# Low parts of the weights of a hybrid encoder layer, granules 10 to 99: an accumulating DMA in place of a subtraction

## The chip, the core and the metric

The kernel runs on one NeuronCore of a Trainium2 chip. The metric is the device time of one execution in microseconds (us), given as the median of several runs. Engines are named as in the profile: PE (matrix multiplication), DVE (vector), ACT (scalar), POOL (GpSimd), SP (the queue that issues most DMAs).

## The reference

One layer of an encoder over 512 tokens of width 1024, in float32. What matters here is that nearly all of the work is activations times large weight matrices:

```python
z, xbc, dt_f, dt_b, q, k, v, gates = split_cols(h @ w_in, IN_SPLITS)
y = ssd_chunked(...forward...) + ssd_chunked(...backward...) + d_skip * xh
branch_ssd = gated_group_rmsnorm(y, z, ssd_norm_g) @ w_br_ssd
branch_attn = windowed_gqa_with_sink(q, k, v, sink) @ w_br_attn
x = x + (g_ssd * branch_ssd + g_attn * branch_attn) @ w_out
x = x + cross_attention(rms_norm(x), rms_norm(mem), w_q, w_kv, w_o)
x = x + (silu(h @ w_gate) * (h @ w_up)) @ w_ffn_out
return rms_norm(x, norm_final_g)
```

## The kernel before

Every weight matrix is cut on the host into **granules** of 128 partitions by 1024 elements (512 KB), numbered 0 to 200 in the order in which the program uses them. The multiplications run on a reduced-precision float format (F32R). To keep float32 accuracy a weight w is split into a high part hi (w rounded to F32R) and a low part lo = w - hi, and an activation likewise. `mac` then issues three matmuls for each 128x128 block: high times high (L140), high weight times low activation (L141) and low weight times high activation (L142). A granule of a projection is 8 blocks, so 24 matmuls of 512 columns. The first of them that reads the low part is the third one.

`load` prepares one granule. SP loads it into a `raw` tile (L122). ACT casts `raw` to the high part `whi` (L130). DVE subtracts, `wlo = raw - whi` (L131). Two ranges deviate: for granules 10 to 18 POOL subtracts (`LO_POOL`), and for granules 79 to 88 DVE also makes the cast (`HI_DVE`, L128). There are two `raw` buffers (`RAWB`), and three each of `whi` and `wlo` (`WB`). So granule g writes the buffers of granule g - 3 and can do so once PE has finished that one. `load` is called so that granule g + 2 is written in the program before the step that uses granule g (`LOOK = 2`).

The stages, by granule: 0 to 27 the key and value projections of the memory (w_xv, w_xk, mixed into the next stage), 8 to 76 the state-space branch (four groups of projections, convolution on DVE and ACT, decay rows masked by POOL at L532 and exponentiated by ACT at L539, and the output projection w_bs), 77 to 92 the windowed attention with its projections (about 515 to 690 us of the profile), 93 to 200 the merge, the cross-attention and the feed-forward part.

Within the block, the order of instructions on each engine is set when the program is built, by a scheduler that works from a timeline of its own. Each engine then runs its instructions in that order, each waiting for semaphores of the others. DMAs that POOL issues stand in POOL's order as well.

Of the kernel before, what the change touches and what calls it, by code (L numbers as in the profile page):

```python
# [9 lines left out]
F32 = mybir.dt.float32  # L10
F32R = mybir.dt.float32r
AF = mybir.ActivationFunctionType
ALU = mybir.AluOpType
AX = mybir.AxisListType

P = 128
# [19 lines left out]
V_MIX, V_XAT, V_MEM, V_FFN, V_FIN = 0, 8, 16, 24, 32  # L36
# [15 lines left out]
HALF = 1  # L52
KVB = 2
LO_POOL = range(10, 19)
HI_DVE = range(79, 89)
ZP = 2
ONE = "mrwomomoo"
TWO = "mzmzm"
# [2 lines left out]
SQ_LAST = 2  # L61
XR = 0
RAWB, WB = 2, 3
EL = (2, 4)


# [7 lines left out]
def bidir_hybrid_layer(ctx: ExitStack, tc: tile.TileContext, io, dbg=None):  # L74
    nc = tc.nc
# [37 lines left out]
    def gcol(c):  # L113
        return vec[:, c:c + 1]


    def load(spec, i):
        src, n = spec
        raw = wp.tile([P, 1024], F32, tag="raw", name="raw", bufs=RAWB)
        for h in range(2 if i < HALF else 1):  # L120
            t = slice(512 * h, 512 * h + 512) if i < HALF else slice(0, n)
            nc.sync.dma_start(raw[:, t], src[:, t])  # L122
        hi = wp.tile([P, 1024], F32R, tag="whi", name="whi", bufs=WB)
        lo = wp.tile([P, 1024], F32R, tag="wlo", name="wlo", bufs=WB)
        for h in range(2 if i < HALF else 1):
            t = slice(512 * h, 512 * h + 512) if i < HALF else slice(0, n)
            if i in HI_DVE:
                nc.vector.tensor_copy(hi[:, t], raw[:, t])  # L128
            else:
                nc.scalar.copy(hi[:, t], raw[:, t])  # L130
            (nc.gpsimd if i in LO_POOL else nc.vector).tensor_tensor(lo[:, t], raw[:, t], hi[:, t].bitcast(F32),  # L131
                                                                     op=ALU.subtract)
        return hi, lo
# [62 lines left out]
    st = {}  # L196
# [287 lines left out]
    def group_scan(g):  # L484
# [124 lines left out]
        for t in range(HPG + LAG3 + 1):  # L609
# [6 lines left out]
            if t >= LAG3 + GLAG and (t - LAG3 - GLAG) % 2 == 0:  # L616
                i = (t - LAG3 - GLAG) // 2
                order += [ga[i]] + el[i + 2:i + 3]
            if t in EL:
                order.append(el[EL.index(t)])  # L620
        cut = order.index(ga[SPLIT]) + 1
# [504 lines left out]
    for i, (fn, gr) in enumerate(steps):  # L1126
        if i == cutat:
            blk.close()
        ahead = LOOK if i >= lead else (i - lead + 4) // 2
        while len(ready) < min(len(specs), taken + len(gr) + ahead):  # L1130
            ready.append(load(specs[len(ready)], len(ready)))
        w = ready[taken:taken + len(gr)]
        taken += len(gr)
        fn(*w)
# [96 lines left out]
```

## Time and profile before

| | |
|---|---|
| median of 3 runs | 1307.06 us (1306.88 to 1308.92) |
| the profiled execution | 1304.91 us, span 1303.1 us |
| PE busy | 1251.0 us, 96% of the span |
| DVE, ACT, POOL busy | 772.1, 564.3, 313.2 us |
| mean granted TensorE clock | 0.991 |

The profile is one execution. Its time is 2.15 us under the median of the runs. The span goes from the first to the last instruction, and 1.8 us of the time lie outside it. Times in rows are counted from the start of the span. A share of busy time is an average over stages that differ: the rows further down are therefore taken from the stretch in which granules 10 to 99 are prepared, 45 to 705 us.

### The profile page before, as it was taken

Reading aid. Unit: us, or ns where it says so; the run is one execution under the profiler, and the core shown is the slowest. Engines: PE = TensorE matmul, PEld = TensorE weight load, DVE = VectorE, ACT = ScalarE, POOL = GpSimd, SP = SyncE. Lnnn points to the kernel's source line nnn. Section 1 sums busy time; section 2 is a strip of 40 time slices with the busy share of each in tenths; the row PEclk is TensorE's granted clock in tenths of the full one; section 3 lists DMA queues with packets and bytes.
Section 4 is the critical chain, followed back from the end, with each engine's and each line's share of the span. In section 5 each row is a group of like instructions: output and inputs, shape, how many; then the busy total and the mean of one; then the engine's idle time right before and its main releaser. Section 6 shows DMA issues by size and latency. Waiting matters only on the chain.

```text
span 1303.1 us, 16244 instructions
## 1 busy us (share of the span) xinstructions
PE 1251.0 (96%) x6076; PEld 1011.3 (78%) x6076; DVE 772.1 (59%) x1226; ACT 564.3 (43%) x1062; POOL 313.2 (24%) x259
## 2 busy tenths in 40 slices
PE   6988999999999999999999999999999999999996
PEld 5776678778778688877667888888888888888886
DVE  5874797677778865688874345675444444432323
ACT  6546655365465232358883234444332222222220
POOL 2344552442671732210000002001111111110001
PEclk9998999999999999999999999999999999999998
DMA  6447364445354232330104333422223222333331
GB/s 228 160 119 196 130 188 148 120 153 141 106 153 137 81 114 80 120 97 33 50 27 139 99 103 107 126 65 65 97 92 98 94 98 95 98 98 94 94 97 65
DMA packets 49614, 143.48 MB, mean 110 GB/s; under 512 B 5120, under 2 KB 8576, under 8 KB 49536
## 3 DMA queue, kind: packets, MB, share of 16 engines
q1 hardware_dynamic: 47248, 138.32, 34.7%
q10 hardware_dynamic: 1584, 2.03, 0.5%
q0 software_dynamic: 704, 2.10, 0.4%
q8 instruction: 48, 0.79, 0.3%
q14 instruction: 30, 0.25, 0.1%
HBM read 137.97 MB, written 4.46 MB: 109 GB/s over the span
## 4 chain that ended last, share of the span: by engine, by line
PE 59%; issue 6%; DVE 2%; ACT 1%; POOL 1%; DMA 0%; DVEq 0%; POOLq 0%; ACTq 0%
PE mm L140 18%; PE mm L142 18%; PE mm L141 18%; PE sb L818 1%; PE sb L805 1%; POOL rsw L717 1%; PE sb L992 1%; PE sa L961 1%; PE sa L777 1%; PE sa L779 0%; PE sb L172 0%; PE sb L572 0%; ACT whi L130 0%; PE sb L155 0%; ACT rsw L716 0%
## 5 line engine op out<-in xcount | busy, mean ns | idle before, releaser
L130 ACT CAST whi<-raw 128x1024 fp32r<-128x1024 f32 (+2 forms) x192 | 198.9, 1036 | 452.3 <-PE mm L141 359.4
L140 PE MATMUL mm<-hh,whi 128*128 128x512 f32 x968 | 382.9, 396 | 11.8 <-DVE cvu L409 11.1
L142 PE MATMUL mm<-hh,wlo 128*128 128x512 f32 x968 | 379.9, 393 | 0.0
L141 PE MATMUL mm<-hl,whi 128*128 128x512 f32 x968 | 379.8, 392 | 0.0
L131 DVE TENSOR_TENSOR wlo<-raw,whi 128x1024 fp32r<-128x1024 f32 (+2 forms) x193 | 238.2, 1235 | 145.0 <-ACT whi L130 135.2
L140 PEld LDWEIGHTS mm<-hh,whi 128*128 128x128 f32 x968 | 182.5, 189 | 52.0 <-issue 8.0
L142 PEld LDWEIGHTS mm<-hh,wlo 128*128 128x128 f32 x968 | 182.4, 188 | 38.9 <-issue 1.8
L141 PEld LDWEIGHTS mm<-hl,whi 128*128 128x128 f32 x968 | 182.7, 189 | 37.1 <-issue 1.1
L539 ACT ACTIVATE rt<-rt,nb 128x128 f32<-128x128 f32 x256 | 78.8, 389 | 67.4 <-POOL rt L532 67.3
L187 POOL TENSOR_TENSOR sq_acc<-sq_acc,sq 128x512 f32<-128x512 f32 x14 | 24.4, 1744 | 259.0 <-ACT sq L186 259.0
L1045 POOL TENSOR_TENSOR fa<-fa,row 128x512 f32<-128x512 f32 x22 | 39.1, 1779 | 192.3 <-ACT fa L1044 192.3
L140 PE MATMUL mm<-vh,whi 128*128 128x512 f32 (+1 forms) x192 | 71.1, 370 | 6.8 <-DVE cvu L409 2.7
L409 DVE SCALAR_TENSOR_TENSOR cvu<-mm,hcw,cvu 128x510 f32<-128x510 f32 (+1 forms) x96 | 71.4, 743 | 5.3 <-ACT cvu L406 3.8
L140 PE MATMUL mm<-fh,whi 128*128 128x512 f32 (+1 forms) x198 | 72.4, 366 | 0.0
L141 PE MATMUL mm<-fl,whi 128*128 128x512 f32 (+1 forms) x198 | 72.4, 365 | 0.0
L142 PE MATMUL mm<-fh,wlo 128*128 128x512 f32 (+1 forms) x198 | 72.4, 365 | 0.0
L142 PE MATMUL mm<-vh,wlo 128*128 128x512 f32 (+1 forms) x192 | 70.7, 368 | 0.0
L141 PE MATMUL mm<-vl,whi 128*128 128x512 f32 (+1 forms) x192 | 68.8, 358 | 0.0
L532 POOL TENSOR_SCALAR_AFFINE_SELECT rt<-rt 128x512 f32<-128x512 f32 x64 | 47.6, 766 | 67.7 <-DMA rt<-adr 67.5
L1047 DVE TENSOR_TENSOR ft<-fa,mm 128x512 f32<-128x512 f32 x22 | 15.1, 688 | 72.5 <-PE mm L142 70.4
L141 PE MATMUL mm<-ol,whi 128*128 128x512 f32 x128 | 50.0, 391 | 0.0
L142 PE MATMUL mm<-oh,wlo 128*128 128x512 f32 x128 | 50.0, 391 | 0.0
(231 smaller groups left out, 1953.7 us busy)
## 6 DMA issues: line engine op xcount, KB each, us to landing
raw<-in_w_in SPq DMA_DIRECT2D x69, 512.0 KB, 3.5
raw<-in_w_fi SPq DMA_DIRECT2D x44, 512.0 KB, 3.5
rt<-adr SPq DMA_DIRECT2D x32, 512.0 KB, 5.5
ear<-edr SPq DMA_DIRECT2D x32, 256.0 KB, 4.5
raw<-in_w_bs SPq DMA_DIRECT2D x16, 512.0 KB, 3.4
raw<-in_w_fo SPq DMA_DIRECT2D x16, 512.0 KB, 3.5
raw<-in_w_xk SPq DMA_DIRECT2D x8, 512.0 KB, 3.9
raw<-in_w_ba SPq DMA_DIRECT2D x8, 512.0 KB, 3.4
```

The lines of the kernel that those rows point to most:

```text
L130: nc.scalar.copy(hi[:, t], raw[:, t])
L131: (nc.gpsimd if i in LO_POOL else nc.vector).tensor_tensor(lo[:, t], raw[:, t], hi[:, t].bitcast(F32), op=ALU.subtract)
L140: nc.tensor.matmul(acc, wh, xh[:, k0 + k], start=first and k == 0, stop=False)
L141: nc.tensor.matmul(acc, wh, xl[:, k0 + k], start=False, stop=False)
L142: nc.tensor.matmul(acc, wl, xh[:, k0 + k], start=False, stop=last and k == nk - 1)
L187: eng.tensor_tensor(acc, acc, sq, op=ALU.add)
L409: nc.vector.scalar_tensor_tensor(u[:, b], acc[:, a], w5[j], u[:, b], op0=ALU.mult, op1=ALU.add)
L532: nc.gpsimd.affine_select(out=rt[:, d].rearrange("p (c l) -> p c l", c=NCH), in_=rt[:, d].rearrange("p (c l) -> p c l", c=NCH), pattern=[[ ...
L539: nc.scalar.activation(r, r, AF.Exp, bias=st["nb"][:, c, e0:e0 + 1])
L717: nc.gpsimd.tensor_tensor(sw, sw, st["ca"][:, S:2 * S], op=ALU.mult)
L1045: nc.gpsimd.tensor_tensor(a, a, st["row2"], op=ALU.mult)
L1047: nc.vector.tensor_tensor(t, a, st["fp", 2 * j + 1], op=ALU.mult)
```

## The change

Granules 10 to 99 (`LO_DMA`) get their low part in another way. ACT makes the high part as before (now L128). A second ACT instruction (L129) writes the negated value, rounded to F32R in the same way, into `wlo`. Then POOL issues a DMA (L133) that reads the granule a second time from device memory and adds it to `wlo` in place, so that `wlo` becomes w - hi. `LO_POOL` is no longer reached, and `HI_DVE` is emptied, so that the casts of granules 79 to 88 return to ACT. For granule 88 (`CHECKED`) the subtraction is also made on DVE for 256 columns, the two are compared, and the largest squared difference times 1e15 is added to the gain of the final norm. Granules 0 to 9 and 100 to 200 stay as they were.

```diff
-HI_DVE = range(79, 89)
+HI_DVE = range(0)
...
+LO_DMA = range(10, 100)
+CHECKED = 88
...
         hi = wp.tile([P, 1024], F32R, tag="whi", name="whi", bufs=WB)
         lo = wp.tile([P, 1024], F32R, tag="wlo", name="wlo", bufs=WB)
+        if i in LO_DMA:
+            nc.scalar.copy(hi[:, :n], raw[:, :n])
+            nc.scalar.activation(lo[:, :n], raw[:, :n], AF.Copy, scale=-1.0)
+            if i == CHECKED:
+                gap = st["at"].tile([P, 256], F32, tag="gap", name="gap", bufs=1)
+                nc.vector.tensor_tensor(gap, raw[:, 0:256], hi[:, 0:256].bitcast(F32), op=ALU.subtract)
+            nc.gpsimd.dma_start(lo[:, :n], src[:, :n], accum_op=ALU.add)
+            if i == CHECKED:
+
+                worst = st["at"].tile([P, 1], F32, tag="worst", name="worst", bufs=1)
+                nc.vector.tensor_tensor(gap, gap, lo[:, 0:256].bitcast(F32), op=ALU.subtract)
+                nc.scalar.activation(gap, gap, AF.Square)
+                nc.vector.tensor_reduce(worst, gap, axis=AX.X, op=ALU.max)
+                nc.vector.scalar_tensor_tensor(gcol(V_FIN), worst, 1e15, gcol(V_FIN), op0=ALU.mult, op1=ALU.add)
+            return hi, lo
```

The scheduler makes a new order of it. The first place is POOL's queue where granules 10 to 16 are prepared. Before, after the four stores of `vdr`, the low parts are subtractions:

```order
L279 DMA vdr_73<-xw_401 128x512
L131 TENSOR_TENSOR wlo_419<-raw_416,whi_418 128x1024
L131 TENSOR_TENSOR wlo_502<-raw_499,whi_501 128x1024
L131 TENSOR_TENSOR wlo_543<-raw_540,whi_542 128x1024
L259 DMA kdr_72<-xw_571 128x256
L131 TENSOR_TENSOR wlo_577<-raw_574,whi_576 128x1024
L131 TENSOR_TENSOR wlo_625<-raw_622,whi_624 128x1024
```

Of the change, the same place:

```order
L296 DMA vdr_73<-xw_401 128x512
L133 DMA wlo_419<-in_w_xk 128x1024
L133 DMA wlo_503<-in_w_in 128x1024
L276 DMA kdr_72<-xw_574 128x256
L133 DMA wlo_545<-in_w_in 128x1024
L133 DMA wlo_580<-in_w_xk 128x1024
L133 DMA wlo_629<-in_w_in 128x1024
```

Each subtraction has become a DMA that POOL issues, in nearly the same place among the others.

The second place is ACT in the state-space stage, at granules 45 and 46 (`cvu`, `cvt`: the convolution; `xk`: a transposed copy; `zs`, `vh`: the gate). Before:

```order
L130 CAST whi_2412<-raw_2410 128x1024
L406 ACTIVATE cvu_2382<-mm_2357,hcw_412 128x512
L466 COPY xk_2181<-sb_2391 128x4x128
L130 CAST whi_2460<-raw_2458 128x1024
L478 ACTIVATE zs_2441<-mm_2416 128x512
L411 ACTIVATE cvt_2388<-cvu_2382 128x512
```

Of the change:

```order
L128 CAST whi_2447<-raw_2445 128x1024
L423 ACTIVATE cvu_2417<-mm_2392,hcw_412 128x512
L129 ACTIVATE wlo_2448<-raw_2445 128x1024
L483 COPY xk_2213<-sb_2426 128x4x128
L428 ACTIVATE cvt_2423<-cvu_2417 128x512
L128 CAST whi_2496<-raw_2494 128x1024
L495 ACTIVATE zs_2477<-mm_2452 128x512
L129 ACTIVATE wlo_2497<-raw_2494 128x1024
```

Every cast has got a second pass over the granule one ACT instruction behind it.

The third place is DVE at the granule that is compared, where the attention begins (`x1`: the gated branch; `sm0`, `sm1`, `mx`: scores and their maxima), of the change alone:

```order
L132 TENSOR_TENSOR gap_4910<-raw_4904,whi_4906 128x256
L859 SCALAR_TENSOR_TENSOR x1_69<-ts_4901,x1_69 128x512
L798 ISA sm0_4946,mx_4950<-sa_4954,ca_4496 128x256
L798 ISA mx_4950 128x1
L137 TENSOR_TENSOR gap_4910<-gap_4910,wlo_4907 128x256
L798 ISA sm1_4947,mx_4950<-sa_4958,ca_4496 128x256
```

The second `gap` row waits for the DMA of that granule, and three of the four score rows of the first attention block stand behind it.

## Rows read from the trace of the kernel before

**Rows 1.** The page: engines' busy time, and the chain that ended last by engine.
```profile
PE 1251.0 (96%) x6076; PEld 1011.3 (78%) x6076; DVE 772.1 (59%) x1226; ACT 564.3 (43%) x1062; POOL 313.2 (24%) x259
...
PE 59%; issue 6%; DVE 2%; ACT 1%; POOL 1%; DMA 0%; DVEq 0%; POOLq 0%; ACTq 0%
```

**Rows 2.** Stages 45 to 705 us and 585 to 690 us: busy time of engines, clock, DMA.
```profile
core 0: us, PE busy (x) PEld busy (x) DVE busy (x) ACT busy (x) POOL busy (x), PEclk, DMA share, GB/s
45.00:705.00 660.00, 631.95 (x3213) 497.28 (x3213) 486.37 (x823) 348.26 (x751) 230.29 (x196) 0.99 0.40 118
585.00:690.00 105.00, 104.04 (x538) 71.59 (x537) 81.95 (x296) 84.27 (x226) 5.26 (x4) 1.00 0.12 40
```

**Rows 3.** What PE waited for, 45 to 705 us: total, times, longest.
```profile
PE mm L140 <- DVE cvu L409: 13.7, 3, 6.4
PE sb L465 <- DVE xs L412: 2.4, 2, 1.7
...
PE sa L777 <- DVE mx L781: 2.3, 2, 1.9
PE mm L140 <- DVE cvt L642: 2.3, 4, 1.4
...
PE sb L805 <- DVE sm L795: 0.2, 1, 0.2
```

**Rows 4.** Three consecutive matmuls of a projection and the next: start, duration (timeline).
```profile
970.63 0.39 PE L140 MATMUL mm<-hh,whi 128*128 128x512 f32 x1
970.86 0.39 PE L141 MATMUL mm<-hl,whi 128*128 128x512 f32 x1
971.08 0.39 PE L142 MATMUL mm<-hh,wlo 128*128 128x512 f32 x1
971.31 0.39 PE L140 MATMUL mm<-hh,whi 128*128 128x512 f32 x1
```

**Rows 5.** Granule 10: cast, and first matmul of its low part (timeline).
```profile
44.76 1.04 ACT L130 CAST whi<-raw 128x1024 fp32r<-128x1024 f32 x1
51.71 0.28 PE L142 MATMUL mm<-vh,wlo 128*128 128x256 f32 x1
```

**Rows 6.** Granule 11: cast, subtraction on POOL, first matmul of its low part.
```profile
53.35 1.05 ACT L130 CAST whi<-raw 128x1024 fp32r<-128x1024 f32 x1 [2.18 <-PE mm L141]
54.48 2.40 POOL L131 TENSOR_TENSOR wlo<-raw,whi 128x1024 fp32r<-128x1024 f32 x1 [5.78 <-ACT whi L130]
57.24 0.39 PE L142 MATMUL mm<-hh,wlo 128*128 128x512 f32 x1
```

**Rows 7.** Granule 79, cast by DVE, and granule 99: cast, first matmul of low part.
```profile
531.29 0.62 DVE L128 CAST whi<-raw 128x1024 fp32r<-128x1024 f32 x1
534.86 0.39 PE L142 MATMUL mm<-hh,wlo 128*128 128x512 f32 x1
701.14 1.06 ACT L130 CAST whi<-raw 128x1024 fp32r<-128x1024 f32 x1 [3.89 <-PE mm L141]
712.50 0.39 PE L142 MATMUL mm<-hh,wlo 128*128 128x512 f32 x1
```

**Rows 8.** DMA issues: size of each, median us from issue to landing.
```profile
raw<-in_w_in SPq DMA_DIRECT2D x69, 512.0 KB, 3.5
rt<-adr SPq DMA_DIRECT2D x32, 512.0 KB, 5.5
...
kdr<-xw POOLq DMA_DIRECT2D x8, 128.0 KB, 4.5
...
edr<-x SPq DMA_DIRECT2D x1, 128.0 KB, 2.2
```

**Rows 9.** POOL 45 to 705 us, groups by line: busy, mean ns, idle before.
```profile
L532 POOL TENSOR_SCALAR_AFFINE_SELECT rt<-rt 128x512 f32<-128x512 f32 x64 | 47.6, 766 | 67.7 <-DMA rt<-adr 67.5
...
L131 POOL TENSOR_TENSOR wlo<-raw,whi 128x1024 fp32r<-128x1024 f32 x9 | 22.4, 2497 | 25.7 <-ACT whi L130 23.5 <-PE mm L141 2.2
...
L259 POOL DMA_DIRECT2D kdr<-xw x8 | 4.5, 563 | 5.5 <-DVE xw L258 5.3 <-issue 0.2
```

**Rows 10.** The subtraction L131, 45 to 705 us: busy time on DVE and POOL.
```profile
45.00:705.00 660.00, 103.92 (x81) 22.40 (x9) 0.99 0.40 118
```

**Rows 11.** DVE ahead of one of PE's three waits for the convolution (timeline).
```profile
111.84 1.23 DVE L131 TENSOR_TENSOR wlo<-raw,whi 128x1024 fp32r<-128x1024 f32 x1 [1.74 <-ACT whi L130]
112.98 0.74 DVE L409 SCALAR_TENSOR_TENSOR cvu<-mm,hcw,cvu 128x510 f32<-128x510 f32 x1
```

## The prediction

> **What bounds the kernel now.** I read the page's busy times and chain first. PE is busy for 1251.0 of 1303.1 us and carries 59% of the chain that ended last; no other engine carries more than 2% [rows 1]. So the kernel runs at the pace of PE, and another engine matters only where PE waits for it. In the stretch in which granules 10 to 99 are prepared, PE is busy for 631.95 of 660 us and DVE for 486.37, the most of the others [rows 2]. The list of PE's waits there shows how much of the rest is DVE's: eight kinds of waits, of which the first and the last stand in [rows 3], 24.8 us in all, over half of it in three waits for the convolution. That sum is the ceiling of what a freer DVE can give back.
>
> Then I read how early a low part has to be there. PE starts a matmul every 0.227 us (970.63 to 971.31 is three) [rows 4], so a granule of 24 takes 5.44 us. The buffers of granule g come free at the end of granule g - 3. The third matmul of granule g comes two granules and 0.45 us later, at least 11.3 us. Granule 99 shows it: its cast starts at 701.14, as soon as PE lets the buffer go, and its low part is first read at 712.50, which is 10.3 us after the cast's end [rows 7]. Other PE work between two granules makes this longer, and a late cast makes it shorter. I went through the timeline and took for each of the 90 granules the time from the end of its cast to the first matmul that reads its low part; call it A. Granule 10 is the first, with 51.71 - 45.80 = 5.9 us [rows 5], granule 99 the last. The shortest are granule 11 with 2.8 us [rows 6] and granule 79 with 2.95 us [rows 7]. The quartiles are 8.4, 11.0 and 14.9 us. Today the subtraction uses 1.3 us of it on DVE (103.92 / 81) and 2.5 us on POOL [rows 9, 10].
>
> **The change part by part.** *DVE* loses 81 subtractions, 103.9 us [rows 10], and ten casts of 0.62 us like that of granule 79 [rows 7]. What that gives is bounded by 0 and the 24.8 us. Where PE waited 6.4 us for the convolution at 113 us, the subtraction stood directly ahead of it but took 1.23 us of the wait [rows 11]. So I take 1.2 us for each of the three long waits and about 2 us for the short ones: 6 us gained.
>
> *ACT* gets 90 negated copies of the cast's size, 1.04 us each [rows 5], and the ten casts: 90 x 1.04 + 10 x 1.04 = 104 us. Over the stretch it goes from 348 to 452 of 660 us, which PE's work covers. In the attention it is busy for 84.27 of 105 us [rows 2]; there about nine granules bring 9.4 us, and the exponentials that PE waits for stand in the same queue. Bounds 0 and 9.4 us; I take 3 us lost. In the order shown, one other ACT instruction stands between a cast and its negated copy, so the copy costs little more than itself.
>
> *POOL* loses nine subtractions (22.4 us) and gets 90 DMA issues of about 0.563 us each, 50.7 us [rows 9]: from 230 to 259 of 660 us. The issues stand in order behind masks of 0.77 us and sums that wait for others. At 39% busy I take 0.5 us of waiting for each, with bounds 0 and 1. In the order shown for granules 10 to 16 the issues stand where the subtractions stood.
>
> *The comparison* of granule 88 adds five small instructions. Its second DVE row waits for one transfer, with three score rows behind it; the granule has over 12 us until its use and I cost it at nothing. Without that cover it is one transfer, at most some 7 us.
>
> *The accumulating transfer* is the unknown, since no row of before shows one. Call D the time from issue to landing. The nearest rows: 512 KB from device memory, issued by SP, land after 3.5 us; 128 KB issued by POOL need 4.5 us and 128 KB issued by SP 2.2 us [rows 8]. So POOL's way costs some 2.3 us more, which gives 3.5 + 2.3 = 5.8 us for a plain copy of a granule. The add also needs the old content of the tile. Size costs (3.5 - 2.2) us for 384 KB, or 1.7 us for a granule, so a second read in full gives 7.5 us. The low end is 3.5 us, as if POOL's way cost nothing. For the high end I have no row: three reads and writes in turn, each at 3.5 us, would be 10.5 us. The DMA engines are busy for 0.40 of the stretch at 118 GB/s [rows 2]; 47 MB more add 71 GB/s, so their share goes to 0.64, or 0.88 if both reads count. Transfers will meet, as with the 5.5 us of the broadcast rows [rows 8]. I take D = 7.0 us, between 5.8 and 7.5 and nearer to the upper.
>
> The Trainium skill, page "Collectives: The Full Stack", section "The bandwidth ceiling: the fold count and why AG ≠ RS ≠ AR", says that an add inside a transfer costs no time in the adder but two source reads, and so halves the rate; by that rule the upper of the two, 7.5 us, holds. No row here shows such an add.
>
> *The sum of the waits.* A low part now needs the negated copy (1.04), POOL's wait (0.5) and D, 8.5 us in all after the cast. It is late by f = 8.5 - A: for 23 granules, most for 11 (5.7 us), 79 (5.6) and 22 (4.8). Delays do not simply add up. When PE waits at granule g, the casts of the next two already run, so only what exceeds the delay gained since two granules earlier counts: T(g) = the larger of T(g - 1) and T(g - 2) + f(g). Carried over the 90 granules this gives T = 34 us with casts as late as before. For D of 3.5, 5, 6, 8, 10 and 12 us it gives 7, 15, 22, 50, 97 and 154 us. If every cast started as soon as its buffer is free, as granule 99's does, the same sum would be 8 us with D = 7, since the time from free buffer to use is 11.2 us or more for nine granules in ten. The new order lies between: DVE no longer holds up casts and the worst granules were accidents of the old order, but ACT has more to do. I take 20 us, about the middle.
>
> Sum: 20 - 6 + 3 = 17 us, so the profiled execution goes from 1304.9 to about 1322 us. The median lies 2.15 us above that execution: 1307 + 17 = 1324 us.
>
> **The rivals.** (1) *The transfer is hidden.* If D plus POOL's wait stays under about 5 us, or the new order starts the casts early, PE waits 3 to 8 us more at low parts, and the 6 us up to, at best, 15 us of DVE's relief decide: -8 to +2 us, 1299 to 1309. For it: half of the granules have A above 11 us, and the plain load lands in 3.5 us. Against it: POOL's own DMAs land after 4.5 us with a quarter of the bytes [rows 8]. It turns at D of about 5 us.
>
> The Trainium skill, page "DMA: Bandwidth & Descriptors", section "Anatomy of one DMA — SWDGE (gpsimd) path", gives 2.0 us plus the bytes over 436 GB/s for a DMA issued by GpSimd, 3.2 us for a granule as an estimate; by that rule this rival holds. The trace disagrees at the size that it shows: 128 KB take 4.5 us, where the rule gives 2.3.
>
> (2) *The transfer is long.* With D of 10 to 12 us the need exceeds the 11.3 us that two dense granules give, so that PE waits in nearly every projection: 97 to 154 us, 1400 to 1460. For it: both reads and the write could go one after the other, while raw loads share the engines. Against it: the load moves 512 KB within 3.5 us.
>
> (3) *ACT becomes the bound in the attention*, where it goes from 84 to some 94 of 105 us: up to 9.4 us instead of 3, with all else as forecast, 1330. It is inside the forecast's own range.
>
> **How the numbers follow.** The forecast (D of 5 to 9 us, +3 to +65 us) gets 0.46, the hidden transfer 0.32, the long one 0.18, and 0.04 is left for gains and losses that cancel. Within 0.2% (2.6 us) is about what a measurement of this kernel cannot tell from no change. The hidden case falls 0.24 into faster and 0.08 into the same, so: faster 0.24, same 0.12, slower 0.64. The range goes from 1296 us, the hidden case with more of DVE's waits cured, to 1390 us (+83, D of about 9.5), which leaves out most of the long case. The forecast's own range is 1310 to 1372 us.
>
> **What would show it.** L133 issues that land after 6 to 8 us; PE waiting at L142 for DMAs into `wlo`, some 20 us between 45 and 705 us, the most near granules 10 to 13, 22 to 28 and 79; DVE about 110 us and POOL 28 us away from before, down and up; ACT up by 104 us; nothing changed after 720 us. Landings under 5 us, or no such waits, would make it wrong on one side; landings over 10 us on the other.

## The result, and the profile after

The changed kernel takes 1367.74 us (median of four runs, 1359.99 to 1369.8) against 1307.37 us before: a ratio of 1.0447 [1.043, 1.0465], so 60 us slower. The forecast was 1324 us. The sign was right, and the time lies inside the wide range, but the loss is more than three times the 17 us that were forecast.

The page of the profile after: busy times, the DMA queues (packets, MB, share of 16 engines), the chain that ended last, and four of the DMA issues (size, median us to landing).

```profile
PE 1274.1 (93%) x6076; PEld 1026.4 (75%) x6076; DVE 664.5 (49%) x1139; ACT 660.6 (48%) x1163; POOL 348.6 (26%) x340
...
q1 hardware_dynamic: 47248, 138.32, 33.5%
q0 software_dynamic: 13664, 49.29, 19.6%
...
PE 64%; DMA 16%; issue 9%; POOL 5%; DVE 3%; ACT 2%; SPq 0%; POOLq 0%; DVEq 0%; ACTq 0%
...
raw<-in_w_in SPq DMA_DIRECT2D x69, 512.0 KB, 5.1
wlo<-in_w_in POOLq DMA_DIRECT2D x63, 512.0 KB, 7.6
...
rt<-adr SPq DMA_DIRECT2D x32, 512.0 KB, 6.8
```

Read PE first. It runs the same 6076 matmuls as before, yet is busy for 1274.1 us where it was 1251.0 [rows 1]. The span went from 1303.1 to 1365.2 us, 62.1 more: 23.1 us are matmuls that took longer, and 39.0 us are idle time (91.1 against 52.1). So there are two losses, and the forecast had terms for the second kind only. DMA has 16% of the chain now; the chain of before can't be set beside it, since its shares in [rows 1] add up to only 69% of the span. The accumulating transfer lands after 7.6 us, near the 7.0 that were taken; the plain loads, 3.5 us before [rows 8], need 5.1.

What PE waited for, 45 to 765 us, which is the work of 45 to 705 us before (total, times, longest). It answers to [rows 3].

```profile
PE mm L159 <- DMA wlo<-in_w_in: 25.1, 13, 4.6
PE mm L159 <- DMA wlo<-in_w_xk: 9.0, 4, 4.4
PE mm L157 <- DVE cvt L659: 6.7, 4, 3.8
PE sa L577 <- ACT cvu L423: 5.9, 1, 5.9
PE sa L794 <- ACT gap L138: 4.7, 1, 4.7
PE sa L577 <- DVE mt L567: 4.1, 2, 3.3
PE sb L460 <- DVE cf L429: 3.6, 1, 3.6
PE sb L515 <- POOL xw L507: 3.4, 2, 3.2
PE mm L157 <- DVE cvu L426: 1.4, 1, 1.4
```

Seventeen waits for low parts make 34.1 us, and the comparison of granule 88 makes 4.7. The waits for the convolution on DVE fell from 13.7 us to 1.4, but other waits took their place, those of L577 for the masked decay rows above all: 10.0 us in three waits, which were 1.0 us before (45 to 705 us):

```profile
PE sa L560 <- DVE mt L550: 1.0, 2, 0.8
```

Without low parts and comparison, 27.1 us are left of PE's 65.9 idle us in this stretch; before it was 660 - 631.95 = 28.05 in all [rows 2].

The stretch as a whole (to be read beside [rows 2]), and 20 us of it in steps of 5 us: busy times of the engines, granted clock, share of the DMA engines, GB/s.

```profile
core 0: us, PE busy (x) PEld busy (x) DVE busy (x) ACT busy (x) POOL busy (x), PEclk, DMA share, GB/s
45.00:765.00 720.00, 654.07 (x3216) 511.41 (x3215) 379.68 (x737) 445.34 (x854) 266.26 (x278) 0.96 0.73 173
...
125.00:130.00 5.00, 5.00 (x34) 4.08 (x32) 0.69 (x1) 1.97 (x5) 1.73 (x3) 1.00 0.76 234
130.00:135.00 5.00, 0.70 (x5) 0.42 (x4) 1.35 (x2) 5.00 (x12) 3.61 (x5) 0.76 0.75 141
135.00:140.00 5.00, 4.90 (x24) 4.83 (x24) 0.00 (x0) 2.07 (x7) 0.97 (x2) 0.55 0.79 189
140.00:145.00 5.00, 3.03 (x10) 2.02 (x9) 2.85 (x4) 3.06 (x7) 2.29 (x3) 0.79 0.58 147
```

The second loss stands here. PE stood still for nearly all of 130 to 135 us, and in the 5 us that followed it was granted 0.55 of its clock, that is 1.2 GHz nearly throughout, and got 24 matmuls done instead of 34. Reading the windows in steps of 2 us, I found ten such places between 45 and 765 us, each at a wait of PE, and three in the kernel before. The clock that was not granted adds up to 29.0 us against 6.8. Part of that falls into the waits themselves and costs nothing: over the time in which PE was busy it is 23.2 us against 4.9. The difference, 18.3 us, is most of the 22.1 us by which PE's busy time grew in the stretch (654.07 against 631.95); the other 3.8 us stay open. Of the 23.2 us, 9.6 lie at five of the waits for low parts, 2.5 at the comparison and 11.2 at four other waits (5.9, 3.6, 3.3 and 3.8 us in the list above); the 4.9 us of before lie at its three waits for the convolution.

Two of the seventeen waits, from the timeline after: granule 21 (cast, negated copy, a mask on POOL, the issue, PE's wait) and granule 79.

```profile
118.66 1.05 ACT L128 CAST whi<-raw 128x1024 fp32r<-128x1024 f32 x1
119.61 1.06 ACT L129 ACTIVATE wlo<-raw 128x1024 fp32r<-128x1024 f32 x1
...
128.28 1.22 POOL L549 TENSOR_SCALAR_AFFINE_SELECT rt<-rt 128x512 f32<-128x512 f32 x2 [5.83 <-DMA rt<-adr]
129.44 0.87 POOL L133 DMA_DIRECT2D wlo<-in_w_xk  x1
...
135.10 0.58 PE L159 MATMUL mm<-vh,wlo 128*128 128x256 f32 x1 [4.41 <-DMA wlo<-in_w_xk]
...
569.63 1.05 ACT L128 CAST whi<-raw 128x1024 fp32r<-128x1024 f32 x1 [7.57 <-POOL x L660]
570.59 1.05 ACT L129 ACTIVATE wlo<-raw 128x1024 fp32r<-128x1024 f32 x1
...
571.93 0.88 POOL L133 DMA_DIRECT2D wlo<-in_w_in  x1 [2.71 <-ACT wlo L129]
...
580.22 0.80 PE L159 MATMUL mm<-hh,wlo 128*128 128x512 f32 x1 [3.25 <-DMA wlo<-in_w_in]
580.81 0.63 PE L157 MATMUL mm<-hh,whi 128*128 128x512 f32 x1
581.24 0.63 PE L158 MATMUL mm<-hl,whi 128*128 128x512 f32 x1
```

The transfer was quick for granule 21: 5.7 us from issue to use. But its copy was ready at 120.67 and the issue came at 129.44, since POOL's queue stood before a mask that waited for a broadcast row. For granule 79 POOL was prompt (0.3 us); there ACT stood 7.57 us before the cast, the last 4.0 of them with the buffer already free, and the transfer then took 8.3 us. The last two rows show 1.2 GHz behind the wait: a matmul every 0.43 us instead of 0.227 [rows 4].

I did this for all seventeen. Four of 1.3 to 4.4 us (granules 21, 22, 25, 27) had 5 to 9 us in POOL's queue; five (10, 18, 48, 79, 84) had a cast 4 to 7 us after the buffer was free; granule 42 had both. These ten make 26.8 of the 34 us. The ten casts that went back to ACT (granules 79 to 88) have no run of their own; five of the seventeen waits, 9.4 us, stand there.

### The profile page after: what moved, and what is told of

It reads as the page before. It is cut to its first block, busy times and chain, and to the rows that moved or that the text cites. A ratio compares the mean times of both kernels' runs of the same rounds, so it can differ in the third digit from the quotient of the medians.

```text
span 1365.2 us, 16370 instructions
## 1 busy us (share of the span) xinstructions
PE 1274.1 (93%) x6076; PEld 1026.4 (75%) x6076; DVE 664.5 (49%) x1139; ACT 660.6 (48%) x1163; POOL 348.6 (26%) x340
## 4 chain that ended last, share of the span: by engine, by line
PE 64%; DMA 16%; issue 9%; POOL 5%; DVE 3%; ACT 2%; SPq 0%; POOLq 0%; DVEq 0%; ACTq 0%
PE mm L159 19%; PE mm L157 19%; PE mm L158 19%; DMA rt<-adr 7%; DMA wlo<-in_w_in 6%; POOL mt L562 1%; DMA raw<-in_w_in 1%; POOL x L660 1%; PE sb L589 1%; PE sb L1009 1%; PE sa L978 1%; POOL rt L549 1%; POOL wlo L133 1%; PE sb L515 1%; PE sb L835 1%
## 5 line engine op out<-in xcount | busy, mean ns | idle before, releaser
L159 PE MATMUL mm<-hh,wlo 128*128 128x512 f32 x968 | 385.0, 398 | 25.1 <-DMA wlo<-in_w_in 25.1
L147 ACT CAST whi<-raw 128x1024 fp32r<-128x1024 f32 (+2 forms) x112 | 115.2, 1029 | 361.5 <-PE mm L158 312.3
L148 DVE TENSOR_TENSOR wlo<-raw,whi 128x1024 fp32r<-128x1024 f32 (+2 forms) x112 | 134.3, 1201 | 101.8 <-ACT whi L147 97.4
L128 ACT CAST whi<-raw 128x1024 fp32r<-128x1024 f32 x90 | 94.2, 1047 | 138.1 <-PE mm L158 86.5
L133 POOL DMA_DIRECT2D wlo<-in_w_in x63 | 55.1, 875 | 169.8 <-ACT wlo L129 126.3
L129 ACT ACTIVATE wlo<-raw 128x1024 fp32r<-128x1024 f32 x90 | 94.6, 1051 | 0.1
L157 PE MATMUL mm<-vh,whi 128*128 128x512 f32 (+1 forms) x192 | 74.4, 388 | 8.2 <-DVE cvt L659 6.7
L158 PE MATMUL mm<-vl,whi 128*128 128x512 f32 (+1 forms) x192 | 72.0, 375 | 0.0
L549 POOL TENSOR_SCALAR_AFFINE_SELECT rt<-rt 128x512 f32<-128x512 f32 x64 | 43.3, 710 | 80.4 <-DMA rt<-adr 80.4
```

What stands on the lines that cost most here:

```text
L128: nc.scalar.copy(hi[:, :n], raw[:, :n])
L129: nc.scalar.activation(lo[:, :n], raw[:, :n], AF.Copy, scale=-1.0)
L133: nc.gpsimd.dma_start(lo[:, :n], src[:, :n], accum_op=ALU.add)
L157: nc.tensor.matmul(acc, wh, xh[:, k0 + k], start=first and k == 0, stop=False)
L158: nc.tensor.matmul(acc, wh, xl[:, k0 + k], start=False, stop=False)
L159: nc.tensor.matmul(acc, wl, xh[:, k0 + k], start=False, stop=last and k == nk - 1)
```

## The experiments

All but e7, e8, e10 and e12 start from the changed kernel without the comparison (e1). "Idle" is span minus PE busy, each from its own page; PE has 6076 matmuls in every run. "Low parts" is what PE waited for the transfers.

| run | median, us | before, us | ratio | span | PE busy | idle | low parts |
|---|---|---|---|---|---|---|---|
| the change | 1367.74 | 1307.37 | 1.0447 [1.043, 1.0465] | 1365.2 | 1274.1 | 91.1 | 34.1 |
| e1 no comparison | 1361.07 | 1309.19 | 1.0386 [1.0348, 1.0423] | 1360.2 | 1274.1 | 86.1 | 32.8 |
| e2 plain transfer | 1330.79 | 1309.19 | 1.0167 [1.0145, 1.0188] | 1333.4 | 1265.9 | 67.5 | 12.9 |
| e3 nobody waits | 1386.52 | 1309.19 | 1.0593 [1.0576, 1.0609] | 1384.1 | 1282.2 | 101.9 | 0 |
| e4 no second read | 1303.88 | 1309.19 | 0.996 [0.9945, 0.9975] | 1301.6 | 1254.0 | 47.6 | 0 |
| e5 low parts last | 1342.6 | 1309.63 | 1.0254 [1.0236, 1.0272] | 1339.2 | 1265.6 | 73.6 | 21.6 |
| e6 negated on DVE | 1345.97 | 1309.63 | 1.0285 [1.0261, 1.0309] | 1342.2 | 1267.3 | 74.9 | 27.7 |
| e7 granules 56 to 78 | 1319.11 | 1309.63 | 1.0078 [1.0061, 1.0095] | 1317.3 | 1258.5 | 58.8 | 8.1 |
| e8 granules 101 to 198 | 1314.77 | 1309.63 | 1.004 [1.0024, 1.0055] | 1312.8 | 1259.3 | 53.5 | 0.2 |
| e9 16 columns only | 1322.79 | 1307.76 | 1.0113 [1.0098, 1.0128] | 1318.9 | 1257.2 | 61.7 | 12.2 |
| e10 before, low last | 1309.87 | 1307.76 | 1.0014 [1.0, 1.0028] | 1308.9 | 1254.1 | 54.8 | 0 |
| e11 e5 and e6 | 1323.84 | 1307.76 | 1.0123 [1.0108, 1.0138] | 1321.9 | 1261.0 | 60.9 | 10.1 |
| e12 granules 12 to 20 | 1313.46 | 1307.76 | 1.0046 [1.0029, 1.0062] | 1311.4 | 1257.4 | 54.0 | 9.8 |

**e1.** The comparison alone.

```diff
-CHECKED = 88
+CHECKED = -1
```

> The changed kernel without the comparison of granule 88; all else as in the change. Theory A (late low parts: what was lost is PE's own waits for the transfers into the low parts, 33 us, and the granted clock that falls after such waits, about 21 us) gives the comparison the one wait of 4.7 us that PE has behind it in the trace, so 1361 to 1364 us. Theory B (crowded transfers: the second read slows all other transfers, and masks, rows and raw loads come late) says the same here. If the comparison were worth 10 us or more, it would be a cause of its own.

Measured 1361.07 us, as both expected. The comparison costs some 7 us by the medians (8 by the ratios): the wait of 4.7 us and what comes behind it. The size is not sharp, since the runs overlap (1359.99 to 1369.8 with it, 1354.67 to 1365.22 without). By the first read of each low part, PE falls a further 8.1 us behind the kernel before between granules 84 and 99 in the change and 2.2 us in e1, a difference of 5.9.

**e2.** Same order on every engine as e1, same bytes from device memory, no add.

```diff
-nc.gpsimd.dma_start(lo[:, :n], src[:, :n], accum_op=ALU.add)
+nc.gpsimd.dma_start(lo[:, :n], src[:, :n].bitcast(F32R))
```

> As the run without the comparison, with the same order of instructions on every engine, but the transfer that POOL issues writes the granule into the low part instead of adding it, so the low part holds the whole weight. Same issue, same bytes from device memory, no read of the tile. If the add is what makes the transfer long and the DMA engines full, landing falls from 7.6 to about 5 us, the share of the DMA engines from 0.75 to about 0.6, and by theories A and B 20 to 40 us come back: 1320 to 1345 us. If instead the place of the issue in POOL's queue decides (theory C: the issue stands behind masks that wait for broadcast rows, up to 8.8 us after the negated copy), less than 10 us come back: 1352 to 1362 us.

Measured 1330.79 us: 30 us are back, within the 20 to 40 of theories A and B and over the 10 of theory C. The page of e1, and then that of e2:

```profile
q0 software_dynamic: 13664, 49.29, 19.5%
...
raw<-in_w_in SPq DMA_DIRECT2D x69, 512.0 KB, 5.1
wlo<-in_w_in POOLq DMA_DIRECT2D x63, 512.0 KB, 8.0
```

```profile
q0 software_dynamic: 13664, 49.29, 10.8%
...
raw<-in_w_in SPq DMA_DIRECT2D x69, 512.0 KB, 3.7
wlo<-in_w_in POOLq DMA_DIRECT2D x63, 512.0 KB, 4.7
```

With the add the same packets kept the DMA engines busy for 19.5% of 1360.2 us, or 265 us; without it 10.8% of 1333.4, or 144 us. The add makes the same packets 1.8 times as much work for the engines and the landing of a transfer 1.6 times as long (7.7 against 4.7 us, the median of all 90), and the plain loads beside it take 5.1 us instead of 3.7. The low-part waits fall from 32.8 to 12.9 us, PE's busy time by 8.2 us, and all other idle time goes from 53.3 to 54.6 us. So what it costs is in the waits for low parts and in slower matmuls; the slower loads show in no other wait. Two things this run doesn't separate: how much of a transfer's length is the add itself and how much the fuller DMA engines, and the add from the conversion of float32 to F32R inside the transfer, which the edit takes out with it.

The Trainium skill, page "Collectives: The Full Stack", section "The bandwidth ceiling: the fold count and why AG ≠ RS ≠ AR", says of ReduceScatter, a transfer between cores that adds, that the add needs two source reads and that it runs at half the rate of a copy. By the engines' busy time the transfer here comes near that (1.8); by the time to landing it is less (1.6). The skill's page "DMA: Bandwidth & Descriptors", section "Anatomy of one DMA — SWDGE (gpsimd) path", gives 3.2 us (an estimate from its formula) for a plain transfer of this size issued by GpSimd; the trace disagrees, with 4.7 and no landing under 3.7.

**e3.** No reader of the low parts.

```diff
-            return hi, lo
+            return hi, hi
```

> No comparison; negated copies and accumulating transfers as in the change, but the third matmul of granules 10 to 99 reads the high part, so the low part that arrives is not used and no engine waits for it. PE does the same number of matmuls. Theory A: PE's waits for low parts (33 us) and the clock lost behind them are gone, and the time is 1300 to 1318 us. Theory B: the other transfers are still slowed, masks and raw loads are still late, and the time stays at 1335 us or more. The scheduler makes a new order for it, since it no longer sees the wait.

Measured 1386.52 us, slower than the change, which by the letter speaks for theory B. The trace says that it tells nothing of the question. Without a reader the scheduler put the negated copies far earlier. ACT's waits, 45 to 745 us:

```profile
ACT wlo L129 <- DMA raw<-in_w_in: 119.8, 34, 7.7
ACT wlo L129 <- DMA raw<-in_w_bs: 45.5, 13, 7.0
```

ACT stood there for 165 us with its convolution and exponentials in the queue behind. It is a new stall, made by the edit; e5 and e11 take up the question.

**e4.** The transfer alone is taken out.

```diff
-            nc.gpsimd.dma_start(lo[:, :n], src[:, :n], accum_op=ALU.add)
```

> No comparison and no accumulating transfer: the low part keeps the negated high part. Casts and negated copies on ACT as in the change, no subtraction on DVE or POOL. All theories that lay the loss on the transfers (A, B, C) expect it at or under the kernel before: 1296 to 1308 us, the prediction's 6 us of relief less 3 us for ACT being 1304. If the ten casts and ninety negated copies on ACT are what costs (theory D), it stays above 1320 us.

Measured 1303.88 us, a ratio of 0.996. This is what theories A, B and C expected; theory D's load on ACT does not by itself bring 1320 us. Freer DVE and POOL, less ACT's load, are together worth 5 us, where the forecast had 6 - 3 = 3. What ACT's copies cost by themselves the run doesn't show apart from that relief.

**e5.** The same transfers, but a later need.

```diff
 for k in range(nk):
     nc.tensor.matmul(acc, wh, xh[:, k0 + k], ...)
     nc.tensor.matmul(acc, wh, xl[:, k0 + k], ...)
-    nc.tensor.matmul(acc, wl, xh[:, k0 + k], ...)
+for k in range(nk):
+    nc.tensor.matmul(acc, wl, xh[:, k0 + k], ...)
```

> No comparison; in every granule the eight matmuls with the low part are issued after the sixteen with the high part, so that a low part is first read 3.2 to 3.6 us later. Transfers as in the change. Theory A (the loss is PE's waits for late low parts, 33 us in seventeen waits of 0.3 to 4.8 us in the run without the comparison, and the clock that falls after the long ones): most of these waits end, under 10 us are left, and the time is 1312 to 1335 us. Theory B (the second read slows all transfers, so masks, rows and raw loads come late, which this does not change): 1345 us or more.

Measured 1342.6 us, between the two. 18 us came back, but 21.6 us of waits are left, not under 10, most of them at other granules than in e1. (The waits of e1, 32.8 us, are fifteen; seventeen is the number in the change.)

**e6.** The negated copy on another engine.

```diff
-nc.scalar.activation(lo[:, :n], raw[:, :n], AF.Copy, scale=-1.0)
+nc.vector.tensor_scalar(lo[:, :n], raw[:, :n], -1.0, None, op0=ALU.mult)
```

> No comparison; the negated copy is made by DVE instead of ACT, beside the cast and not behind it. Theory D (ACT: its copies make casts late, 4 to 9 us after the buffer is free for granules 10, 42, 48, 79 and 84, and the negated copy ends 2.0 to 4.5 us after the cast's start): the waits for low parts fall from 33 to about 15 us and the time to 1330 to 1345 us. If only the transfer and POOL's queue count, at most the 1.3 us by which the copy ends earlier is gained per wait: 1345 to 1358 us.

Measured 1345.97 us, at the border of the two. 15 us came back, as theory D has it, but the waits fell only to 27.7 us: four of the five over 3 us went, that of granule 79 grew from 3.0 to 5.2 us, and short ones came in. PE's busy time fell by 6.8 us. So only 5 of the 15 us are waits for low parts, and that ACT's copies made the casts late is shown only in part.

**e7.** Part of the change on the kernel before (`HI_DVE` as before).

```diff
+LO_DMA = range(56, 79)
```

> The kernel before, with the accumulating transfer for granules 56 to 78 only (23 of the 90). In the trace of the change PE is as far behind the kernel before at granule 79 (41.5 us) as at granule 56 (41.9), so by theory A, whose waits stand elsewhere, this costs nothing: within 3 us of the kernel before. By theory B in the form that each second read costs the same wherever it is, a quarter of the loss: 13 to 16 us slower.

Measured 1319.11 us, 9.5 us slower: theory A's number was wrong. PE's waits for low parts in it, from the timeline, are 2.7 us at granule 57, 0.9 at 58 and 4.5 at 62. In the full change PE waited for none of these three low parts, which landed 6.0, 1.8 and 2.2 us before their use. I put that down to PE having been held up before; the order of the program differs too, and no run separates the two. Where a chain has waits, the place at which none shows is not one that is free.

**e8.** The last part of the program, with more granules than the change has.

```diff
+LO_DMA = range(101, 199)
```

> The kernel before, with the accumulating transfer for granules 101 to 198 only, the merge, the cross-attention and the feed-forward part (98 granules, more than the change has). PE has no broadcast rows or masks to wait for there, and the DMA engines are busy for 0.30 of it. Theory A with the lead of 11.3 us and a need of 2.0 us for cast and copy, 0.3 for POOL and 6 to 7.6 for the transfer: hidden, within 4 us of the kernel before, with some loss possible in the cross-attention. Theory B in the form that each second read costs the same: 50 us or more slower.

Measured 1314.77 us, 5.1 us slower (3 to 7 by the interval) where theory A had up to 4 and theory B over 50. Two stretches of it, and two DMA issues of its page:

```profile
1000.00:1100.00 100.00, 100.00 (x443) 82.84 (x442) 19.34 (x28) 46.61 (x56) 27.50 (x27) 1.00 0.91 194
1100.00:1200.00 100.00, 100.00 (x442) 82.65 (x441) 15.89 (x23) 44.39 (x53) 26.43 (x27) 1.00 0.90 191
```

```profile
raw<-in_w_fi SPq DMA_DIRECT2D x44, 512.0 KB, 6.5
wlo<-in_w_fi POOLq DMA_DIRECT2D x44, 512.0 KB, 7.6
```

The DMA engines are busier here than in the change (0.91 against 0.73) and loads land after 6.5 us, yet PE is busy throughout at 2.4 GHz. By the first matmul of each granule, PE is 4.2 us behind the kernel before already at granule 100, and until about there every engine has the same order as before; from there to granule 200 the 98 transfers add 3.0 us.

**e9.** The same issue and wait, few bytes.

```diff
-nc.gpsimd.dma_start(lo[:, :n], src[:, :n], accum_op=ALU.add)
+nc.gpsimd.dma_start(lo[:, :16], src[:, :16], accum_op=ALU.add)
```

> No comparison; the accumulating transfer covers 16 of the 1024 columns, so it has the same issue on POOL, behind the same masks, and the same wait of PE, but 1/64 of the bytes (the other columns of the low part keep the negated high part). With POOL's queue alone (theory C: waits of 5 to 9 us in front of the issue for granules 20 to 28 and 41, 42) most of the 13 us of waits of the run with the plain read stay, and the time is 1318 to 1330 us. If the bytes decide (theories A and B: the length of the transfer and the crowding of the DMA engines), it is within 8 us of the run without a second read, 1304 to 1312 us.

Measured 1322.79 us, as theory C expected: 19 us more than without any transfer, though these land after 3.5 us. The timeline of e9 for granule 22:

```profile
126.97 1.06 ACT L129 ACTIVATE wlo<-raw 128x1024 fp32r<-128x1024 f32 x1
...
130.65 1.23 POOL L549 TENSOR_SCALAR_AFFINE_SELECT rt<-rt 128x512 f32<-128x512 f32 x2 [6.24 <-DMA rt<-adr]
...
140.29 1.23 POOL L549 TENSOR_SCALAR_AFFINE_SELECT rt<-rt 128x512 f32<-128x512 f32 x2 [5.05 <-DMA rt<-adr]
141.47 0.86 POOL L133 DMA_DIRECT2D wlo<-in_w_in  x1
...
143.90 0.77 PE L159 MATMUL mm<-hh,wlo 128*128 128x512 f32 x1 [5.35 <-DMA wlo<-in_w_in]
```

The copy was ready at 128.03, the issue came 13.4 us later, and the transfer took 2.4 us. The order of the program is a new one, so not all of the 19 us need be POOL's queue. Of the 12.2 us of waits for low parts, 6.7 stand behind 8 to 13 us in that queue (granules 17, 21 and 22); at granules 11, 48 and 86, 5.5 us, the copy waited at most 0.9 us there. PE's busy time is 3.2 us longer than in e4.

**e10.** e5's edit of the matmuls on the kernel before.

> The kernel before with the low-part matmuls last in each granule, as a control of the run that did this to the change. PE waits there for low parts for only 1.3 us, so if that run gained its 18 us by the later need, nothing is to be gained here: 1303 to 1310 us. If the new order of the program was what gained, this is 10 us or more faster than the kernel before, under 1298 us.

Measured 1309.87 us, no gain. The edit by itself makes no better order, so I put e5's gain down to the later need; e5's own order, which is new too, has no control.

**e11.** e5 and e6 together.

> No comparison; accumulating transfers as in the change, with the low-part matmuls last and with the negated copies on DVE. Each alone took 15 to 18 us off the 1361 us. Theory A (lateness is a sum of cast, copy, POOL's queue and transfer, set against a lead): both together take off 25 to 35 us, 1325 to 1336 us, with under 12 us of waits for low parts left. If both gained only by the new order, the second adds nothing: 1340 to 1350 us.

Measured 1323.84 us: 37 us back of the 52 by which e1 is slower, with 10.1 us of low-part waits. All 90 accumulating transfers are still there, and the DMA engines are as busy as in the change (0.75 from 45 to 734 us). All that is left in e11, crowding included, is the 16 us by which it is slower than the kernel before, or 20 us against e4. What crowding is worth where the lead is short, as in e1, that doesn't show.

**e12.** The early part, on the kernel before.

```diff
+LO_DMA = range(12, 21)
```

> The kernel before with the accumulating transfer for granules 12 to 20 only. In the run without the comparison PE waits for none of these nine low parts, and in the run without any second read PE is 12 us ahead of the kernel before at granule 20, since POOL's subtractions of 2.5 us and DVE's are gone. Theory A: up to 12 us of that relief stay, 1297 to 1307 us. If even nine transfers slow the broadcast rows and raw loads enough (theory B), or the relief is lost again by the end as it was in the run without any second read, 1307 to 1315 us.

Measured 1313.46 us, against theory A's number. PE waits 4.2, 3.6 and 2.0 us at granules 12, 18 and 20, where e1 showed no waits: the mistake of e7 again. No version here that computes the whole result beats the kernel before.

## Why the prediction was right in sign and wrong in size

Worked out in the stretch 45 to 705 us before and 45 to 765 us after, the 60 us are: low parts 34.1, comparison 4.7, all other waits 27.1 - 28.05 = -0.9, slower matmuls 654.07 - 631.95 = 22.1. The sum is 60.0. The forecast was 20 - 6 + 3.

The step that failed is this sum. It counts a wait of PE at its length and has no term for matmuls that get slower, which came to 22.1 of the 43 us that it missed. Its term for the waits for low parts was 20 us and measured 34.1, and the comparison, put at nothing, made PE wait 4.7 us. The mechanism, low parts that come too late, is the one forecast.

- **PE paces the kernel, DVE is relieved.** Right, though the chain of [rows 1] that it leaned on covers only 69% of the span. DVE fell by 107.6 us (772.1 to 664.5; forecast 110). The relief less ACT's price is 5 us by e4. With the transfers in, it is given back inside "other waits": 12.3 us less for the convolution, about as much more elsewhere.
- **ACT.** The size was right (445.34 - 348.26 = 97 us, forecast 104). The price was in the wrong place. In e4 none shows, but with transfers behind it six of the seventeen waits have a cast 4 to 9 us after the free buffer, at five of them with other work of ACT just ahead; e6 gains 15 us, of which 5 are such waits.
- **POOL.** A size out of its bounds: "I take 0.5 us of waiting for each, with bounds 0 and 1". Over the 90 granules it was 1.36 us on average (122 us in all), but 5 to 9 us at the granules named above, and up to 13.4 us in e9. POOL is busy for 266 of 720 us; what holds the issue is a mask that itself waits for a DMA. The trace before had it: 67.5 us of waiting ahead of the masks [rows 9]. An average from a busy share can't show it. An issue takes 0.87 us, not 0.563; the plain one of e2 takes 0.57.
- **The comparison at nothing.** Wrong by some 7 us, the very price that was named for the case without cover. The 12 us until the granule's own use were no cover for the score rows behind it, which PE needs much sooner. DVE stood 5.8 us before the second row (timeline after):

```profile
638.73 0.42 DVE L137 TENSOR_TENSOR gap<-gap,wlo 128x256 f32<-128x256 f32 x1 [5.77 <-DMA wlo<-in_w_in]
```

- **The transfer.** Right: D is 7.6 us against 7.0. Single ones took 5.4 to 11.2 us, the longest more than the high end of 10.5. The engines' share of 0.73 lies between 0.64 and 0.88. The add costs 30 us (e2), the largest step that one edit took back in the same order.
- **The sum of the waits.** 20 us forecast, 34.1 measured, as much as the same sum gave "with casts as late as before". That is luck, for need and lead were both longer than assumed. From the end of the cast to the landing it took 10.1 us (median, mean 10.9) where 8.5 were taken; carried by the same rule over the leads of before, the measured needs would give 95 us. The lead A, the waits taken off, has quartiles of 10.9, 12.7 and 17.5 us where it had 8.4, 11.0 and 14.9. So the reason for going to the middle, that casts would start earlier, held for most: half of them start within 0.1 us of the free buffer (2.2 before), and of granules 12 to 99 16 come 4 us late or more (29 before). It did not hold at the six late ones among the seventeen waits. The places were half right: granules 10, 11, 22, 25, 27 and 79 were named (12 us), but 21, 42, 48 and 84 (16 us) were not.
- **The clock.** Slower matmuls were missing altogether, the largest error: 22 us, of which the granted clock explains 18.3. Of the eleven waits over 3 us between 45 and 765 us nine have a stretch at 1.2 GHz at their end or within 2 us behind it; at the other two (3.2 us at 161, 3.1 at 615) the clock stayed at 2.4 GHz. With the clock counted, low parts cost 34.1 + 9.6 = 43.7 us, the comparison 4.7 + 2.5 = 7.2, and the other waits -0.9 + 11.2 - 4.9 = 5.4.
- **Rivals.** The hidden transfer fell with D of 7.6 us; it is true in the feed-forward part (e8). The long one fell with the same number. ACT in the attention did not bind PE by its exponentials (0.2 us of PE's waits there are ACT's, apart from the comparison), but five waits for low parts, 9.4 us, stand there. That crowding of the DMA engines slows everything (theory B) is real in the landings. That it is not where most of the time went is supported, not proven: PE's waits other than for low parts are together no longer in e1 than in e2 (53.3 and 54.6 us), e8 is hidden at 0.91, and e11 takes back 37 us under the same load.

As steps, over the kernel before and by the medians: without transfers -5 us (e4), a tiny transfer in POOL's queue +15 (e9), the whole granule plainly +22 (e2), the add +52 (e1), the comparison +60. Only e1 and e2 have the same order on every engine. Open stays how much of the step to e9 is POOL's queue and how much its new order.

## What to carry to other kernels

A chain that replaces one instruction has as many queues in it as it has engines; look in the trace for what stands ahead at each one, and for waits on DMAs above all, and not for the engine's busy share. Count a wait of PE of some microseconds at more than its length, since the clock fell at nine of the eleven over 3 us here: 39 us more of idle time came with 23 us of slower matmuls. And a granule that shows no wait behind others that do is not proof that it would have none alone.

## What was unexpected of the hardware

- At waits of 2 to 6 us PE was granted 1.2 GHz for some 3 to 10 us, ten times between 45 and 765 us of the changed kernel. DMA load alone did not do it: at 0.91 of the DMA engines the clock stayed at 2.4 GHz while PE had work (e8).
- An accumulating transfer keeps the DMA engines busy 1.8 times as long as a plain one (265 against 144 us for the queue, e1 and e2), and POOL needs 0.87 us to issue it against 0.57, also when it has only 16 columns.
